# Latent attention's scores in a two-layer backbone: from 96-row products, head after head, to 64-row products of two heads side by side

## The chip, the cores and the metric

The kernel runs on one core of one Trainium2 chip. The metric is device time in microseconds for one execution; the time before is 1802.9 us, the median of three runs (1801.73 to 1808.01). Besides its five engines (PE multiplies matrices, DVE and ACT work on vectors, POOL is a slower vector engine, SP issues transfers) the text speaks of the tile shape of a matmul, as the trace writes it: `128*128` uses all 128 rows of the array for the contraction, `64*128` only one half of them, so that two such products can stand in it together.

## What is computed

A backbone of two layers over 512 latent tokens and 256 context tokens, width 1024. Each layer: a modulated norm, one input projection whose columns go to four groups (neighbourhood attention, sliding window attention, latent attention, state space), an output projection, then a modulated norm and an MLP of 4096 with squared ReLU. In the second layer the context stream is not carried on. Latent attention, cut to what matters (4 heads; 64 features without position, 32 rotary ones that all heads share on the key's side):

```python
cq, ckv, kr = split(p, [256, 384])
q  = rmsnorm(cq, g_q) @ w_uq            # per head: qn (64), qr (32)
kv = rmsnorm(ckv, g_kv) @ w_ukv         # per head: kn (64), v (64)
qr, kr = axial_rope(qr, ang), axial_rope(kr, ang)   # latent tokens only
s = (einsum('bqhd,bkhd->bhqk', qn, kn) + einsum('bqhd,bkd->bhqk', qr, kr)) * 96 ** -0.5
o = softmax(s) @ v                      # 128 queries at a time
```

## The kernel before

**Products in two parts.** To keep the accuracy of float32 with the faster number format, nearly every operand is split in a high and a low part (in the code `h` and `l`: `wh`, `wl`, `ah`, `al`), and a product is three matmuls: high by high, low by high, high by low. `dense()` does so for all projections and the MLP. It takes the weights of 128 output columns, splits them (high part on ACT, low part on DVE), and runs 8 matmuls for each of the three passes and each segment: segment 0 are the 512 latent tokens, segment 1 the 256 context tokens.

**Order.** The kernel is written in Python generators, one for each group, that are merged; a scheduler of the toolchain then orders each engine's instructions by its own estimates, except where `tc.issue_after` chains two. So the text of the program does not fix the place of an instruction. Banks for scores come from a pool (`pss`), those for transposes and dense products from another (`pst`).

**Latent attention** is `mla()`. It loads its weights by POOL's queue, norms `ckv` and `cq`, turns the rotary key (`krr`, all 32 features of a token beside each other), and then makes the queries in three blocks of 128 columns: two blocks hold two heads' position-free parts each, the third the rotary parts of all four heads (rows 32 by 32). Scaled copies on ACT and, for the rotary part, four 32-row additions on DVE put them in `qh[hd]`, one tile of 96 rows a head: 64 position-free, 32 rotary. The keys go the same way into `kh[hd]` and `kl[hd]`: the rotary key is transposed and written to rows 64 to 96 of all four heads, the position-free part to rows 0 to 64, each time by `put_k`, with a copy on ACT (high) and a subtraction on DVE (low). There are 16 of each in a layer. `split_q` makes high and low of the query block (ACT, POOL).

**A score block** is 128 queries of one head against the 512 latent and the 256 context keys (context queries, in the first layer only: 256 context keys). `attend()` takes the two heads of a pair together. For latent attention it runs all scores of the first head, then all of the second: three matmuls of 96 rows each for 512 and for 256 columns. For the other two attentions (`paired=True`) the heads' 64-row products alternate, chained with `issue_after`. Then, head by head: minimum over the scores on DVE, exponential on ACT, reciprocal and scaling; the probabilities are transposed by PE, 128 columns at a time (L473), copied, and multiplied with the values in a 128x64 shape (L479). A layer has two pairs of heads and 4 or (first layer) 6 blocks.

**The MLP's start.** The MLP begins for the latent half before the context half of the norm is through (in the second layer: for the first 256 tokens before the second 256). `rest` is the generator with what is left of output projection and norm; `NAHEAD` up blocks (3 and 5) are computed for the first half alone; in the middle of the first one, and a few times after each (`PACE`, 6), one step of `rest` is placed. Its last steps are the norm's: sums of squares (L296), the reciprocal root on DVE, the broadcast of it over the partitions (L308), and the modulation: `xn`, high part `ah`, low part `al` for each of the 8 tiles of 128 features.

Of the kernel before, what the change touches and what calls it, by code (L numbers as in the profile page):

```python
# [72 lines left out]
QORD = (0, 1, 2)  # L73
# [18 lines left out]
def kernel(ctx: ExitStack, tc: tile.TileContext, D: dict, out: bass.AP, dbg=None):  # L92
# [157 lines left out]
    def dense(src, acts, segs, evac, ks=range(KD), w=None, low=V, midway=None):  # L250
# [139 lines left out]
    def attend(q, k, parts, sinks, vt, put, sgn=-1.0, paired=False):  # L390
# [14 lines left out]
        if paired:  # L405


            off, prev = 0, None
            for k0, n, tab in parts:
                if off == 0 or off + n - b0 > 512:  # L410
                    banks, b0 = (pss(), pss()), off
                dst = [banks[a][:, off - b0:off - b0 + n] for a in range(2)]
                nmm = len(terms(0))
                for i in range(nmm):
                    for a in range(2):
                        x, y = terms(a)[i]
                        with (tc.issue_after(prev.ins) if prev else nullcontext()):
                            prev = PE.matmul(dst[a], x, y[:, k0:k0 + n], start=i == 0, stop=i == nmm - 1)  # L418
                for a in range(2):
                    ats[a].append((dst[a], off, n, tab))  # L420
                off += n
        else:
            for a in range(2):
                off = 0
                for k0, n, tab in parts:
                    if off == 0 or off + n - b0 > 512:
                        bank, b0 = pss(), off
                    dst = bank[:, off - b0:off - b0 + n]
                    mm = terms(a)
                    for i, (x, y) in enumerate(mm):  # L430
                        PE.matmul(dst, x, y[:, k0:k0 + n], start=i == 0, stop=i == len(mm) - 1)  # L431
                    ats[a].append((dst, off, n, tab))
                    off += n
# [205 lines left out]
    for l in range(DEPTH):  # L639
# [329 lines left out]
        def mla():  # L969
# [36 lines left out]
            for b in range(4):  # L1006
# [4 lines left out]
            qh = [unit("u", nm("qh")) for _ in range(4)]  # L1011
            kh = [(unit("u", nm("kh"), F32R), unit("u", nm("kl"), F32R)) if SR[2] else unit("u", nm("kh"))
                  for _ in range(4)]

            def put_k(hd, r0, r1, c0, n, ps):
                if not SR[2]:
                    evac(kh[hd][r0:r1, c0:c0 + n], ps)
                    return
                hi, lo = (x[r0:r1, c0:c0 + n] for x in kh[hd])
                A.copy(hi, ps)  # L1020
                V.tensor_tensor(lo, ps, hi.bitcast(F32), ALU.subtract)

            vm = [unit("u", nm("vm")) for _ in range(2)]

            def queries():
                msc = -(96.0 ** -0.5)
                for b in QORD:
                    for s, c0, n in segs:
# [4 lines left out]
                        if b < 2:  # L1033
                            for e in range(2):
                                A.activation(qh[2 * b + e][0:64, c0:c0 + n], ps[64 * e:64 * e + 64, :n], AF.Copy, scale=msc)
                        elif s == 1:
                            for hd in range(4):
                                A.activation(qh[hd][64:96, c0:c0 + n], ps[32 * hd:32 * hd + 32, :n], AF.Copy, scale=msc)
                        else:
                            qr, qs = unit("q", nm("qr")), unit("q", nm("qs"))  # L1040
                            A.activation(qr[:, :SEQ], ps, AF.Copy, scale=msc)
# [4 lines left out]
                            for hd in range(4):  # L1046
                                rs_ = slice(32 * hd, 32 * hd + 32)
                                V.tensor_tensor(qh[hd][64:96, 0:SEQ], qr[rs_, :SEQ], qs[rs_, :SEQ], ALU.add)
# [4 lines left out]
            for s, c0, n in full:  # L1053
                pk = pss()
                for t in range(n // P):
                    PE.transpose(pk[0:32, t * P:(t + 1) * P], krr[:, c0 // P + t, :], ident)
                for hd in range(4):
                    put_k(hd, 64, 96, c0, n, pk[0:32, 0:n])
            yield
            for b in range(2):  # L1060
                for s, c0, n in full:
                    ps = pss()
                    PE.matmul(ps[:, :n], wkv[:, b * P:(b + 1) * P], ckv[:, c0:c0 + n], start=True, stop=True)
                    for e in range(2):
                        put_k(2 * b + e, 0, 64, c0, n, ps[64 * e:64 * e + 64, :n])
# [8 lines left out]
            for b in range(2):  # L1074
                om = unit("u", nm("om"))
                for j in range(WS // P):
# [7 lines left out]
                    qs = [qh[2 * b + a][0:96, cs] for a in range(2)]  # L1084
                    ks = [kh[2 * b + a] for a in range(2)]
                    if SR[2]:
                        qs = [tuple(x[0:96] for x in split_q(x, 96)) for x in qs]
# [381 lines left out]
```

## Time and profile before

| what | value |
|---|---|
| median of 3 runs | 1802.9 us (1801.73 to 1808.01) |
| the profiled execution | 1802.71 us, of which the span 1800.9 |
| PE busy | 1750.6 us, 97% of the span |
| DVE, ACT, POOL busy | 1109.4, 737.8, 240.3 us |
| latent scores (L431) | 216 matmuls: 96 of 512 columns, 120 of 256 |

How to read it: a line of the timeline gives an instruction's start and length in us, then the engine, the line of the code, the operation, what it writes and reads, its tile shape and sizes, how many alike follow, and, in brackets, how long the engine was idle before it and what ended that. Matmuls are pipelined: one's start lies ahead of the end of the one before, so the price of one is the distance between two ends (start plus length) or between two starts, not its length. In the windows the granted clock is 1.00 for 2.4 GHz and 0.50 for 1.2 GHz.

### The profile page before, as it was taken

How to read it: one execution, taken by the hardware profiler on the slowest of the kernel's cores; microseconds unless marked ns; L12 is line 12 of the kernel's file. 1: busy time of each engine (PE TensorE's matmuls, PEld its weight loads, DVE VectorE, ACT ScalarE, POOL GpSimd, SP SyncE). 2: the span in 40 equal slices, each digit the busy share in tenths (PEclk: the TensorE clock that was granted, in tenths of full speed). 3: DMA queues.
4: the chain of work that ended last, by engine and by line, in shares of the span. 5: the costliest groups of instructions: out<-in, count | busy, mean ns of one | idle time of the engine just before them, and what ended most of it. 6: DMA issues, size and time to landing. Idle time of an engine off the chain costs nothing.

```text
span 1800.9 us, 28892 instructions
## 1 busy us (share of the span) xinstructions
PE 1750.6 (97%) x11170; PEld 1493.3 (83%) x11170; DVE 1109.4 (62%) x2372; ACT 737.8 (41%) x1497; POOL 240.3 (13%) x367
## 2 busy tenths in 40 slices
PE   8999999999989999999999999999989999999998
PEld 7877877777878888888888998688878898888888
DVE  5548458688677566467555674757779563444355
ACT  4347546655353123123123443545544451323244
POOL 0102011234320000000000331101114310000002
PEclk8999999999999999999999999899999999999999
DMA  9440267632635445344444534111333543222333
GB/s 337 138 152 17 67 214 248 214 115 93 211 109 177 136 153 163 109 154 144 155 135 146 173 113 138 35 36 36 120 110 104 199 146 100 94 94 94 106 104 119
DMA packets 86249, 238.94 MB, mean 133 GB/s; under 512 B 9200, under 2 KB 17392, under 8 KB 86112
## 3 DMA queue, kind: packets, MB, share of 16 engines
q1 hardware_dynamic: 74976, 208.57, 35.8%
q0 software_dynamic: 7104, 24.33, 3.8%
q10 hardware_dynamic: 4032, 4.20, 0.7%
q8 instruction: 88, 1.44, 0.3%
q14 instruction: 49, 0.40, 0.1%
HBM read 214.52 MB, written 22.54 MB: 132 GB/s over the span
## 4 chain that ended last, share of the span: by engine, by line
PE 89%; DVE 6%; DMA 2%; ACT 1%; issue 1%; POOL 0%; DVEq 0%; ACTq 0%; POOLq 0%; SPq 0%
PE pt L261 68%; PE pt L479 3%; PE pt L473 3%; PE pS L666 2%; PE pS L431 2%; PE pS L418 2%; PE pt L172 1%; PE pt L666 1%; PE pt L296 1%; PE pt L933 1%; PE pS L1031 1%; DVE pr L441 1%; DVE wl L239 1%; PE pt L864 0%; DMA old<-in_hT_dram 0%
## 5 line engine op out<-in xcount | busy, mean ns | idle before, releaser
L238 ACT CAST wh<-wr 128x1024 fp32r<-128x1024 f32 x206 | 215.9, 1049 | 403.0 <-PE pt L261 291.2
L239 DVE TENSOR_TENSOR wl<-wr,wh 128x1024 fp32r<-128x1024 f32 x206 | 253.9, 1233 | 100.5 <-ACT wh L238 96.0
L261 PE MATMUL pt<-ah,wh 128*128 128x512 f32 (+1 forms) x1304 | 275.0, 352 | 7.1 <-ACT ah L346 3.1
L261 PE MATMUL pt<-al,wh 128*128 128x512 f32 (+1 forms) x1304 | 269.5, 347 | 0.0
L261 PE MATMUL pt<-ah,wl 128*128 128x512 f32 (+1 forms) x1304 | 268.7, 348 | 0.0
L261 PEld LDWEIGHTS pt<-ah,wh 128*128 128x128 f32 x1304 | 213.3, 190 | 48.0 <-ACT ah L346 4.3
L261 PEld LDWEIGHTS pt<-ah,wl 128*128 128x128 f32 x1304 | 215.2, 191 | 31.4 <-issue 0.8
L261 PEld LDWEIGHTS pt<-al,wh 128*128 128x128 f32 x1304 | 212.9, 190 | 31.1 <-issue 2.4
L261 PE MATMUL pt<-hh,wh 128*128 128x256 f32 (+1 forms) x896 | 168.2, 330 | 0.0
L261 PE MATMUL pt<-hl,wh 128*128 128x256 f32 (+1 forms) x896 | 167.0, 329 | 0.0
L261 PE MATMUL pt<-hh,wl 128*128 128x256 f32 (+1 forms) x896 | 166.9, 329 | 0.0
L1291 DVE SCALAR_TENSOR_TENSOR h<-pt,mod,h 128x512 f32<-128x512 f32 (+1 forms) x112 | 66.3, 595 | 153.8 <-PE pt L261 153.6
L261 PEld LDWEIGHTS pt<-hh,wh 128*128 128x128 f32 x896 | 137.6, 189 | 17.7 <-issue 0.6
L261 PEld LDWEIGHTS pt<-hh,wl 128*128 128x128 f32 x896 | 138.0, 190 | 15.4
L261 PEld LDWEIGHTS pt<-hl,wh 128*128 128x128 f32 x896 | 138.1, 190 | 15.0
L208 DVE SCALAR_TENSOR_TENSOR ma<-wm,cact,ma 128x768 f32<-128x768 f32 x112 | 109.9, 1013 | 65.3 <-DMA wm<-in_w_mod_dram 65.2
L1281 ACT ACTIVATE r<-pt 128x512 f32<-128x512 f32 (+1 forms) x101 | 51.4, 509 | 237.1 <-PE pt L261 237.1
L1283 DVE TENSOR_TENSOR r<-r 128x512 f32<-128x512 f32 (+1 forms) x101 | 58.2, 577 | 123.0 <-ACT r L1281 122.9
L322 POOL TENSOR_TENSOR sq<-sq,sq 128x256 f32<-128x256 f32 x66 | 64.7, 980 | 442.9 <-ACT sq L318 442.2
L455 ACT ACTIVATE pr<-pr,m 128x512 f32<-128x512 f32 (+2 forms) x96 | 77.8, 811 | 40.3 <-DVE m L441 38.4
L261 PE MATMUL pt<-oh,wo 128*128 128x256 f32 (+1 forms) x576 | 93.9, 306 | 0.0
L261 PEld LDWEIGHTS pt<-oh,wo 128*128 128x128 f32 x576 | 79.0, 194 | 5.5 <-issue 1.7
(295 smaller groups left out, 2473.5 us busy)
## 6 DMA issues: line engine op xcount, KB each, us to landing
wr<-in_w_mlp_dram SPq DMA_DIRECT2D x154, 512.0 KB, 3.5
wo<-oscr SPq DMA_DIRECT2D x66, 512.0 KB, 4.7
wm<-in_w_mod_dram SPq DMA_DIRECT2D x80, 384.0 KB, 3.6
wr<-in_w_a_dram SPq DMA_DIRECT2D x36, 512.0 KB, 4.1
wm<-in_w_mod_dram SPq DMA_DIRECT2D x32, 512.0 KB, 4.0
wr<-in_w_out_dram SPq DMA_DIRECT2D x16, 512.0 KB, 4.3
oscr<-wh POOLq DMA_DIRECT2D x16, 512.0 KB, 3.7
oscr<-wl POOLq DMA_DIRECT2D x16, 512.0 KB, 5.6
```

What stands on the lines that cost most here:

```text
L208: V.scalar_tensor_tensor(a[:, :T], w, cact[:, k, i:i + 1], a[:, :T], ALU.mult, ALU.add)
L238: A.copy(wh, raw)
L239: low.tensor_tensor(wl, raw, wh.bitcast(F32), ALU.subtract)
L261: PE.matmul(ps[:, :n], w[:, k - k0, :], acts[k][a][:, c0:c0 + n], start=i == 0, stop=i == len(mm) - 1)
L322: G.tensor_tensor(sq[0][:, :n], sq[0][:, :n], q[:, :n], ALU.add)
L455: A.activation(pr[:, :off], src, AF.Exp, scale=-1.0 if tabs else sgn, bias=mcol, accum_out=s2[:, a:a + 1])
L473: PE.transpose(pt[:, i * P:(i + 1) * P], probs[a][:, (g0 + i) * P:(g0 + i + 1) * P], ident)
L479: last_mm = PE.matmul(pv[64 * a:64 * a + 64, :P], vt(a, t), pts[a][:, t * P:(t + 1) * P], start=t == 0, stop=t == nkt - 1)
L666: PE.matmul(acc[t], acts[k][a][:, t * P:(t + 1) * P], slabs[pc][w][:, kk, :], start=k == 0 and x == 0, stop=k == KD - 1 and x == 2)
L1281: A.activation(r[:, :n], ps, AF.Relu)
L1283: V.tensor_tensor(r2[:, :n], r[:, :n], r[:, :n], ALU.mult)
L1291: V.scalar_tensor_tensor(h[d][:, c0:c0 + n], ps, mod[:, 40 + d, s:s + 1], h[d][:, c0:c0 + n], ALU.mult, ALU.add)
```

## The change

The position-free parts of two heads stay as the projection gives them, side by side in 128 rows (`qn`, `kn`), and the product of a head reads its 64 rows. The rotary parts get a product of their own: for each head 64 rows that hold 32 of the query's high part above 32 of its low part (`qst`), against the key's high part twice (`kst[0]`) and its low part twice (`kst[1]`). So a block has five 64-row terms a head instead of three 96-row ones, and all attentions now run the paired form, the two heads alternating. `kst` comes from four copies of the rotary key beside each other (`k4`), transposed as 128x128. `qst` is put together by 8 transfers a layer on POOL's queue (`RQ = 0`). The rotary query block is made first (`QORD`). A further part is in the MLP's start: `midway` now names the matmul ahead of which a step of `rest` is placed, the first up block has its step at matmul 12 of 24, the second one at 6 (first layer) or 18 (second), and the steps after the first up block are gone.

```diff
-QORD = (0, 1, 2)
+QORD = (2, 0, 1)
+RQ = 0
 ...
-                if midway and i == len(mm) // 2:
-                    midway()
+                if midway and i == midway[0]:
+                    midway[1]()
 ...
-            return [(q[a][0], k[a][0]), (q[a][1], k[a][0]), (q[a][0], k[a][1])]
+            return [(q[a][0], k[a][0]), (q[a][1], k[a][0]), (q[a][0], k[a][1]), *extra[a]]
 ...
+            k4 = unit("q", nm("k4"))
+            A.copy(k4[:, :T].rearrange("p (t r e) -> p t r e", r=4, e=32),
+                   krr[:, :, None, :].to_broadcast([P, 6, 4, 32]))
+            for s, c0, n in full:
+                pk = pss()
+                for t in range(n // P):
+                    PE.transpose(pk[:, t * P:(t + 1) * P], k4[:, c0 + t * P:c0 + (t + 1) * P], ident)
+                hi, lo = (x[:, c0:c0 + n] for x in kst)
+                A.copy(hi, pk[:, 0:n])
+                V.tensor_tensor(lo, pk[:, 0:n], hi.bitcast(F32), ALU.subtract)
 ...
-                            for hd in range(4):
-                                rs_ = slice(32 * hd, 32 * hd + 32)
-                                V.tensor_tensor(qh[hd][64:96, 0:SEQ], qr[rs_, :SEQ], qs[rs_, :SEQ], ALU.add)
+                            V.tensor_tensor(qr[:, :SEQ], qr[:, :SEQ], qs[:, :SEQ], ALU.add)
+                    if b == 2:
+                        hi, lo = unit("q", nm("qrh"), F32R), unit("q", nm("qrl"), F32R)
+                        A.copy(hi[:, :WS], qr[:, :WS])
+                        V.tensor_tensor(lo[:, :WS], qr[:, :WS], hi[:, :WS].bitcast(F32), ALU.subtract)
+                        for hd in range(4):
+                            for i, x in enumerate((hi, lo)):
+                                r0 = 64 * (hd % 2) + 32 * i
+                                (G, nc.scalar)[RQ].dma_start(qst[hd // 2][r0:r0 + 32, :WS].bitcast(F32),
+                                                             x[32 * hd:32 * hd + 32, :WS].bitcast(F32))
 ...
-                    for e in range(2):
-                        put_k(2 * b + e, 0, 64, c0, n, ps[64 * e:64 * e + 64, :n])
+                    hi, lo = (x[:, c0:c0 + n] for x in kn[b])
+                    A.copy(hi, ps[:, :n])
+                    V.tensor_tensor(lo, ps[:, :n], hi.bitcast(F32), ALU.subtract)
 ...
-                    attend(qs, ks,
-                           part, None, vt, lambda ps, om=om, cs=cs: evac(om[:, cs], ps))
+                    x = split_q(qn[b][:, cs], P)
+                    attend([rows(x, a, slice(0, P)) for a in range(2)], [rows(kn[b], a) for a in range(2)],
+                           part, None, vt, lambda ps, om=om, cs=cs: evac(om[:, cs], ps),
+                           extra=[[(rows(qst[b], a, cs), rows(y, a)) for y in kst] for a in range(2)])
 ...
-                    ahead.append(up_block(qd, f, parts[:1], midway=None if f else lambda: next(rest)))
-                    for _ in range(PACE[l] - (f == 0)):
+                    now = (12, (6, 18)[last], None)[min(f, 2)]
+                    ahead.append(up_block(qd, f, parts[:1], midway=now and (now, lambda: next(rest))))
+                    for _ in range(PACE[l] if f else 0):
                         next(rest, None)
```

The line numbers after the change are a little other than before: L431 becomes L418, L473 L461, L479 L467, L261 L262, L296 L297, L308 L309, L1021 L1052 and L1014.

**PE, latent attention of the first layer, before**: the scores of one head (`kh`, `kl` by `nqh`, `nql`), between transposes of probabilities (`con,pr`) and the product with the values (`vm`).

```order
L473 MATMUL pt_1413<-con,pr_1394 128x128 x4
L473 MATMUL pt_1419<-con,pr_1394 128x128 x2
L1105 MATMUL pt_1440<-sq_1017,con 128x512
L431 MATMUL pS_1612<-kh_1109,nqh_1602 128x512
L431 MATMUL pS_1612<-kh_1109,nql_1603 128x512
L431 MATMUL pS_1612<-kl_1110,nqh_1602 128x512
L473 MATMUL pt_1487<-con,pr_1472 128x128 x4
L479 MATMUL pt_1419<-pT_1401,vm_1117 64x128
```

The same place after: the two heads' banks alternate, `kst,qst` are the rotary terms, and four transposes stand inside the fourth pair of terms, two more behind the fifth.

```order
L418 MATMUL pS_1596<-kh_1107,nqh_1590 128x512
L418 MATMUL pS_1597<-kh_1107,nqh_1590 128x512
L418 MATMUL pS_1596<-kh_1107,nql_1591 128x512
L418 MATMUL pS_1597<-kh_1107,nql_1591 128x512
L418 MATMUL pS_1596<-kl_1108,nqh_1590 128x512
L418 MATMUL pS_1597<-kl_1108,nqh_1590 128x512
L418 MATMUL pS_1596<-kst_1113,qst_1111 128x512
L461 MATMUL pt_1478<-con,pr_1459 128x128 x4
L418 MATMUL pS_1597<-kst_1113,qst_1111 128x512
L418 MATMUL pS_1596<-kst_1114,qst_1111 128x512
L418 MATMUL pS_1597<-kst_1114,qst_1111 128x512
L461 MATMUL pt_1484<-con,pr_1459 128x128 x2
```

Before, transposes stand between whole heads; now a pair of heads is one chain of ten for 512 columns, cut once inside by transposes and once ahead of the 256 columns.

**DVE, latent attention of the second layer, before**: behind the rotation of the query (`qs`, `qr`) come the additions into `qh` and then the keys' low parts, of which the first five are shown.

```order
L1044 TENSOR_TENSOR qs_11680<-pt_11682,sin_11442 128x512
L1045 TENSOR_TENSOR qr_11679<-qr_11679,cos_11441 128x512
L1048 TENSOR_TENSOR qh_11652<-qr_11679,qs_11680 32x512
L1048 TENSOR_TENSOR qh_11653<-qr_11679,qs_11680 32x512
L1048 TENSOR_TENSOR qh_11654<-qr_11679,qs_11680 32x512
L1048 TENSOR_TENSOR qh_11655<-qr_11679,qs_11680 32x512
L1021 TENSOR_TENSOR kl_11657<-pS_11749,kh_11656 32x512
L1021 TENSOR_TENSOR kl_11657<-pS_11762,kh_11656 32x256
L1021 TENSOR_TENSOR kl_11657<-pS_11783,kh_11656 64x512
L1021 TENSOR_TENSOR kl_11659<-pS_11749,kh_11658 32x512
L376 COPY sk_11690<-pt_11723 128x256
L1021 TENSOR_TENSOR kl_11659<-pS_11762,kh_11658 32x256
```

After: the rotary key's low parts (`kst`) come first, then one addition, the rotary query's low part (`qrl`), and four low parts of the keys.

```order
L1014 TENSOR_TENSOR kst_11675<-pS_11680,kst_11674 128x512
L1014 TENSOR_TENSOR kst_11675<-pS_11687,kst_11674 128x256
L1030 TENSOR_TENSOR qs_11693<-pt_11698,sin_11456 128x512
L1031 TENSOR_TENSOR qr_11692<-qr_11692,cos_11455 128x512
L1032 TENSOR_TENSOR qr_11692<-qr_11692,qs_11693 128x512
L1036 TENSOR_TENSOR qrl_11704<-qr_11692,qrh_11703 128x512
L377 COPY sk_11723<-pt_11756 128x256
L240 TENSOR_TENSOR wl_12260<-wr_12257,wh_12259 128x1024
L1052 TENSOR_TENSOR kl_11669<-pS_11782,kh_11668 128x512
L1052 TENSOR_TENSOR kl_11669<-pS_11786,kh_11668 128x256
L1052 TENSOR_TENSOR kl_11671<-pS_11790,kh_11670 128x512
L1052 TENSOR_TENSOR kl_11671<-pS_11794,kh_11670 128x256
```

Four additions became one, and of the 16 subtractions into `kl` four are left, with two into `kst` ahead of the rotation.

**PE, start of the MLP in the first layer, before**: sums of squares (L296) and broadcast (L308) of the norm's second half, between the dense matmuls of the first and second up block.

```order
L261 MATMUL pt_5991<-al_5662,wh_5987 128x512
L296 MATMUL pt_6004<-ones,sq_5825 128x1 x2
L261 MATMUL pt_5991<-al_5664,wh_5987 128x512
L308 MATMUL pt_6037<-con,rs_6009 128x128 x2
L261 MATMUL pt_6066<-ah_5649,wh_6062 128x512
L261 MATMUL pt_6066<-ah_5651,wh_6062 128x512
```

After: the second up block's matmuls stand between the two.

```order
L297 MATMUL pt_6018<-ones,sq_5839 128x1 x2
L262 MATMUL pt_6059<-ah_5663,wh_6055 128x512
...
L262 MATMUL pt_6059<-ah_5669,wh_6055 128x512
L262 MATMUL pt_6005<-al_5678,wh_6001 128x512
L262 MATMUL pt_6059<-ah_5671,wh_6055 128x512
...
L262 MATMUL pt_6059<-al_5676,wh_6055 128x512
L262 MATMUL pt_6059<-al_5678,wh_6055 128x512
L309 MATMUL pt_6066<-con,rs_6023 128x128 x2
L262 MATMUL pt_6127<-ah_5663,wh_6123 128x512
L262 MATMUL pt_6127<-ah_5665,wh_6123 128x512
```

One dense matmul stood between sums and broadcast; now there are 25, the one left of the first up block among them.

## Rows read from the trace of the kernel before

**Rows 1.** the page: busy time by engine, and the chain that ended last

```profile
PE 1750.6 (97%) x11170; PEld 1493.3 (83%) x11170; DVE 1109.4 (62%) x2372; ACT 737.8 (41%) x1497; POOL 240.3 (13%) x367
...
PE 89%; DVE 6%; DMA 2%; ACT 1%; issue 1%; POOL 0%; DVEq 0%; ACTq 0%; POOLq 0%; SPq 0%
```

**Rows 2.** timeline of PE, latent scores of layer 0: start us, length us, instruction

```profile
145.92 0.39 PE L431 MATMUL pS<-kh,nqh 96*128 96x512 f32 x1
...
146.62 0.28 PE L431 MATMUL pS<-kh,nqh 96*128 96x256 f32 x1
...
146.97 0.40 PE L431 MATMUL pS<-kh,nqh 96*128 96x512 f32 x1
...
148.10 0.88 PE L473 MATMUL pt<-con,pr 128*128 128x128 f32 x6
148.73 0.48 PE L431 MATMUL pS<-kh,nqh 96*128 96x512 f32 x1
```

**Rows 3.** timeline of PE, entry and exit of the 64-row tiles in layer 0

```profile
210.45 0.38 PE L418 MATMUL pS<-oh,nqh 64*128 64x256 f32 x1
210.76 0.44 PE L473 MATMUL pt<-con,pr 128*128 128x128 f32 x2
211.13 0.38 PE L418 MATMUL pS<-oh,nqh 64*128 64x256 f32 x1
...
211.71 0.39 PE L418 MATMUL pS<-ol,nqh 64*128 64x256 f32 x2
212.03 1.31 PE L473 MATMUL pt<-con,pr 128*128 128x128 f32 x10
...
227.63 0.27 PE L418 MATMUL pS<-oh,nqh 64*128 64x256 f32 x1
227.83 2.12 PE L261 MATMUL pt<-ah,wh 128*128 128x512 f32 x8
```

**Rows 4.** windows: us, busy us of each engine (instructions), granted clock, DMA share, GB/s

```profile
142.00:200.00 58.00, 57.76 (x450) 46.26 (x449) 46.36 (x141) 41.37 (x107) 13.37 (x28) 1.00 0.15 47
...
1126.00:1153.00 27.00, 24.98 (x92) 15.52 (x92) 17.73 (x28) 13.70 (x29) 2.51 (x7) 0.94 0.19 59
1153.00:1168.00 15.00, 13.31 (x56) 10.40 (x55) 14.88 (x42) 8.05 (x20) 2.85 (x5) 0.77 0.00 1
1425.00:1440.00 15.00, 11.20 (x64) 10.40 (x64) 10.53 (x28) 8.27 (x19) 6.57 (x7) 0.77 0.44 154
```

**Rows 5.** timeline of DVE, layer 1: the low parts of the keys

```profile
1140.87 2.44 DVE L1021 TENSOR_TENSOR kl<-pS,kh 32x512 fp32r<-32x512 f32 x4 [2.21 <-ACT kh L1020]
...
1145.51 5.69 DVE L1021 TENSOR_TENSOR kl<-pS,kh 64x512 fp32r<-64x512 f32 x10
```

**Rows 6.** timeline of PE, layer 1, between the keys and the first latent scores

```profile
1146.35 1.10 PE L1063 MATMUL pS<-ckv,wkv 128*128 128x512 f32 x2 [0.85 <-DVE kl L1021]
1148.46 0.71 PE L1063 MATMUL pS<-ckv,wkv 128*128 128x256 f32 x2 [1.02 <-DVE kl L1021]
```

**Rows 7.** timeline of PE, start of the MLP in layer 0

```profile
516.68 0.43 PE L308 MATMUL pt<-con,rs 128*128 128x128 f32 x2 [3.01 <-DVE rs L288]
516.87 3.18 PE L261 MATMUL pt<-ah,wh 128*128 128x512 f32 x8
...
525.84 1.98 PE L261 MATMUL pt<-ah,wl 128*128 128x512 f32 x8
527.65 1.98 PE L261 MATMUL pt<-al,wh 128*128 128x512 f32 x8
529.47 3.01 PE L261 MATMUL pt<-ah,wh 128*128 128x256 f32 x22
```

**Rows 8.** timeline of DVE, the second half's modulation, MLP of layer 0

```profile
517.23 1.66 DVE L339 SCALAR_TENSOR_TENSOR xn<-h,gsc,pt 128x256 f32<-128x256 f32 x4
...
533.17 0.48 DVE L347 SCALAR_TENSOR_TENSOR al<-xn,mod,ah 128x256 fp32r<-128x256 f32 x1
```

**Rows 9.** DMA issues: KB each, us from issue to landing

```profile
vscr<-vna POOLq DMA_DIRECT2D x12, 128.0 KB, 2.3
```

More of the change, by code (lines that the diff above doesn't have):

```diff
@@ L387, in behind, with attend @@
             fn()
-    def attend(q, k, parts, sinks, vt, put, sgn=-1.0, paired=False):
+    def attend(q, k, parts, sinks, vt, put, sgn=-1.0, extra=((), ())):
         tabs = len(parts) > 1
@@ L401, in terms @@
                 return [(q[a], k[a])]
-            return [(q[a][0], k[a][0]), (q[a][1], k[a][0]), (q[a][0], k[a][1])]
+            return [(q[a][0], k[a][0]), (q[a][1], k[a][0]), (q[a][0], k[a][1]), *extra[a]]
         ats = ([], [])
[L405 to L418, printed above, removed]
+        off, prev = 0, None
+        for k0, n, tab in parts:
+            if off == 0 or off + n - b0 > 512:
+                banks, b0 = (pss(), pss()), off
+            dst = [banks[a][:, off - b0:off - b0 + n] for a in range(2)]
+            nmm = len(terms(0))
+            for i in range(nmm):
                 for a in range(2):
-                    ats[a].append((dst[a], off, n, tab))
-                off += n
-        else:
+                    x, y = terms(a)[i]
+                    with (tc.issue_after(prev.ins) if prev else nullcontext()):
+                        prev = PE.matmul(dst[a], x, y[:, k0:k0 + n], start=i == 0, stop=i == nmm - 1)
             for a in range(2):
[L424 to L433, printed above, removed]
+                ats[a].append((dst[a], off, n, tab))
+            off += n
         for a in range(2):
@@ L1010, in mla @@
             V.tensor_copy(krr[:, 4:6], kr[:, 4:6])
[L1011 to L1021, printed above, removed]
-            vm = [unit("u", nm("vm")) for _ in range(2)]
+            qn = [unit("u", nm("qn")) for _ in range(2)]
+            kn = [(unit("u", nm("kh"), F32R), unit("u", nm("kl"), F32R)) for _ in range(2)]
+            qst = [unit("u", nm("qst"), F32R) for _ in range(2)]
+            kst = [unit("u", nm("kst"), F32R) for _ in range(2)]
+            vm = [unit("u", nm("vm")) for _ in range(2)]
+            k4 = unit("q", nm("k4"))
[8 more added lines that the diff above has]
+                V.tensor_tensor(lo, pk[:, 0:n], hi.bitcast(F32), ALU.subtract)
             def queries():
                 msc = -(96.0 ** -0.5)
+                qr, qs = unit("q", nm("qr")), unit("q", nm("qs"))
                 for b in QORD:
@@ L1032, in queries @@
                                       start=k == 0, stop=k == 1)
-                        if b < 2:
-                            for e in range(2):
-                                A.activation(qh[2 * b + e][0:64, c0:c0 + n], ps[64 * e:64 * e + 64, :n], AF.Copy, scale=msc)
-                        elif s == 1:
-                            for hd in range(4):
[L1038 to L1041, printed above, removed]
+                        dst = qn[b] if b < 2 else qr
+                        A.activation(dst[:, c0:c0 + n], ps[:, :n], AF.Copy, scale=msc)
+                        if b == 2 and s == 0:
                             pp = pst()
@@ L1052, in mla @@
                 yield from queries()
[L1053 to L1059, printed above, removed]
             for b in range(2):
@@ L1063, in mla @@
                     PE.matmul(ps[:, :n], wkv[:, b * P:(b + 1) * P], ckv[:, c0:c0 + n], start=True, stop=True)
-                    for e in range(2):
-                        put_k(2 * b + e, 0, 64, c0, n, ps[64 * e:64 * e + 64, :n])
+                    hi, lo = (x[:, c0:c0 + n] for x in kn[b])
+                    A.copy(hi, ps[:, :n])
+                    V.tensor_tensor(lo, ps[:, :n], hi.bitcast(F32), ALU.subtract)
             yield
@@ L1198, in put @@
                             evac(on[:, cs], ps)
-                    attend([rows(x, a, slice(0, P)) for a in range(2)], [rows(blocks["nk", b], a) for a in range(2)], part, None, vt, put, sgn=1.0, paired=True)
+                    attend([rows(x, a, slice(0, P)) for a in range(2)], [rows(blocks["nk", b], a) for a in range(2)], part, None, vt, put, sgn=1.0)
                     if j == 3:
```

10 lines of the change are left out of this document (1 added, 9 removed).

## Prediction

> **What bounds the kernel now.** I read the page first, then the stretches that the change touches. The page shows PE busy for 1750.6 of the span's 1800.9 us, and the chain that ended last is PE for 89% of its length, DVE for 6% [rows 1]: time is won or lost where PE's own work changes, or where PE waits. The windows then tell which it is in each stretch. During layer 0's latent attention (142 to 200 us) PE is busy 57.76 of 58 us at full clock, while DVE has 46.36 and ACT 41.37: only PE's work counts there. In layer 1, from the latent queries to the early scores (1126 to 1168), PE is busy 24.98 of 27 and 13.31 of 15, and its granted clock averages 0.94 and 0.77; DVE has 14.88 of the last 15 us [rows 4]. There DVE sets the pace, and PE pays twice, by waiting and by running at 1.2 instead of 2.4 GHz afterwards. Two of these waits are named: 0.85 and 1.02 us before the key matmuls, both ended by a low part of the keys (kl) on DVE [rows 6].
>
> **The scores: fewer PE slots.** A latent score block costs, per head, three 512-column and three 256-column matmuls, one after the other. By consecutive starts, three of 512 take 146.62 - 145.92 = 0.70 us, 0.233 each, and three of 256 take 146.97 - 146.62 = 0.35, 0.117 each [rows 2]. The program holds 96 of the first and 120 of the second: 96 x 0.233 + 120 x 0.117 = 36.4 us. Afterwards a pair of heads needs five pairs of 64-row matmuls (three latent terms, two rotary) in place of six single ones: 80 pairs of 512 and 100 pairs of 256. The trace has 64-row pairs of 256 columns: from the end at 211.51 to the end at 212.10 five pairs finish (the rows between are of the same kind, twelve matmuls in all), 0.118 a pair [rows 3]. So the two halves do run side by side, a pair costs what one 96-row matmul costs, and for 512 columns, which no row shows, I take 2 x 0.118 = 0.236 by the nearest row. The bounds are 0.233 (full overlap) and 0.467 (none). Sum: 80 x 0.236 + 100 x 0.118 = 30.7 us, that is -5.7. No overlap for 512 alone would turn this into +12.8; the 256 rows speak against it.
>
> **The scores: more changes of tile shape.** A 64-row tile differs from the 128-row one around it, and the trace prices that. Going in: transposes end at 211.20, the next 64-row matmul of 256 columns ends at 211.51, 0.31 against 0.118, so +0.19. Coming out: from 210.83 to 211.20 two transposes take 0.37, and from 212.10 to 213.34 ten take 1.24; eight more cost 0.87, so 0.109 each, and the exit is 0.37 - 0.22 = +0.15 [rows 3]. Into the dense product, eight matmuls after a 64-row one take 2.05 (227.90 to 229.95), against 1.81 (527.82 to 529.63) among themselves, +0.24 [rows 3, 7]. The 96-row scores of before don't pay it: transposes end at 148.98, the next score of 512 columns at 149.21, 0.23 later, its usual price [rows 2]. The TensorEngine Tiling (Array Packing) page of the Trainium skill, section Key Properties, says that changing the tiling mode drains the engine while changing the tile does not; the exits above agree.
>
> How many more there are the order tells, not the diff: entries from 128x128 into 64x128 go from 55 to 87, exits from 51 to 82, because the scheduler puts two or four transposes between score matmuls, even inside a term. 32 x 0.19 + 31 x 0.15 = +10.7 (with all exits at 0.24 it is +13.5). The rotary key's six transposes now run in the dense shape, 6 x 0.109 = 0.65 instead of 0.82 by before's row of the same stretch, which is 0.3 for both layers. PE's own work: -5.7 + 10.7 - 0.3 = +4.7. Layer 0's half of it is on the path in full, since PE is all that is busy there. With the pairs uncut (20 entries fewer) it would be about -2, with all exits dear about +7.5.
>
> **Layer 1's stretch: less on DVE.** Before, 16 subtractions make the keys' low parts in this layer: the four and ten in the rows, 2.44 + 5.69 us, and two of 256 columns, about 0.42 each by the shorter ones: 9.0 us [rows 5]. Four 32-row additions build the queries. After, four subtractions of 128 rows, two for the rotary key, one addition and one subtraction for the rotary query remain. DVE's price goes by columns: ten of mixed width averaged 0.57, so eight cost about 4.6 us. With the additions DVE loses roughly 7 us of work ahead of the first latent score. What PE can get back is bounded: idle 27 - 24.98 + 15 - 13.31 = 3.7 us, and the slow clock, (1 - 0.94) x 27 + (1 - 0.77) x 15 = 5.1 us, which is what running at half speed lost [rows 4]. So 0 to -8.8. I take the two waits named for kl, 1.9, the first drop of the clock that follows them, 1.6, and a quarter of the remaining 5.3: -5 in round numbers. The other waits are behind softmax, which stays.
>
> **The rotary query's copies.** Eight transfers on POOL's queue stack the query's high and low parts per layer; before has none. The nearest row, a write by the same queue, lands in 2.3 us [rows 9]. Queued behind them are the low parts of the latent queries on POOL. In layer 1's order there are 48 dense matmuls (24 x 0.227 + 24 x 0.12 = 8.3 us), the keys and the values between the rotary product and the first score that reads the stack, so I expect no wait: 0, at worst +3 in layer 1, nothing in layer 0, where sixty more matmuls stand between.
>
> **The MLP's start.** In layer 0 PE now waits 3.01 us for the reciprocal root before its broadcast (L308), then runs slow: the first eight matmuls take 3.18 us where eight later take 1.98, and the 48 from 516.87 to 529.47 need 12.6 us where 48 x 0.227 is 10.9, 1.7 lost [rows 7]. After, 25 dense matmuls stand ahead of the broadcast, so these 4.7 us go. But the second half's modulation, which starts with xn at 517.23, right after the broadcast, and ends with al at 533.65 [rows 8], comes later relative to PE: before, 48 matmuls of 512 columns run between broadcast and the first 256-column one at 529.47, after only 24 (24 x 0.227 = 5.45), plus 2.6 for the 22 that follow. PE reaches the last high part about 8.1 us after the broadcast; it came some 15 us after it, some 14 when one up block less is interleaved on DVE. New wait 5.8: net +1.1, between -4.7 (hidden after all) and +3 (and a new drop of the clock). Layer 1's start already idles, 3.8 of 15 us [rows 4], ahead of its broadcast; 77 matmuls then cover the second half: +0.5, 0 to 1.5.
>
> **Sum.** +4.7 - 5.0 + 0 + 1.1 + 0.5 = +1.3 against the profiled 1802.71 us (span 1800.9 and 1.8 around it), which stands 0.2 under the median of 1802.9: 1804.
>
> **Rivals.** First, clearly faster: layer 1's stretch gives back all 8.8, and the modulation's wait stays hidden (-4.7), with the shape changes partly falling into waits in layer 1 (+3 instead of +4.7): 1802.7 - 10.5 = 1792. For it: both waits are tied to DVE, which loses 7 us. Against it: layer 0 has nothing to hide the changes. The same page's Overview gives up to twice the speed for contraction sizes of 64 or less; five slots for six is all that this trace allows of it.
>
> Second, slower: the pairs delay softmax in layer 1. Before, the first head's scores are complete after 1.05 us (0.70 + 0.35) and its softmax begins while PE makes the second head's; after, both are complete only at 5 x 0.354 = 1.77. Where DVE is saturated (14.88 of 15) and PE has no dense work ready, the chain of each block starts 0.7 later, 8 blocks in layer 1: +5.8, and the -5 doesn't come. 4.7 + 5.8 + 1.1 + 0.5 = +12: 1815. It decides where PE waits after scores for transposes; for it, the stretch is already softmax-bound at its end; against it, the second head is ready 0.3 sooner. The tiling page's section PSUM Bottleneck says that tiling speeds the engine but not the emptying of its banks, by which this rival would be right in layer 1; layer 0's free DVE speaks against it there.
>
> Third, the modulation's wait is worse than costed and drops the clock again, with PE's work at +7.5: 1811, inside the range.
>
> **How the numbers follow.** A measurement of this kernel can tell about 0.5%, 9 us, from no change (1793.9 to 1811.9). My forecast with its own range, 1796 to 1811, gets 0.52; the faster rival 0.25; the slower one 0.16, the third 0.07. Faster by over 0.5%: 0.25; slower by more: 0.16 and a share of the third's, 0.22; within: 0.53. The range from 1791 to 1815 holds all but the far ends.
>
> **What would show it.** Right: latent pairs of 512 columns about 0.236 apart; the first matmul after each change 0.15 to 0.24 longer; the stretch in layer 0 from first to last latent score longer by 2 to 5 us; the waits behind kl gone and the first latent score of layer 1 about 5 us sooner after its queries; at the MLP's start of layer 0 no wait before the broadcast, and new ones for ah or al in the 256-column products. Wrong: a wait of the first rotary score for a transfer, 512-column matmuls that run one after the other, or a clock that drops at new places.

## The result: slower by 0.9%

The changed kernel takes 1819.87 us (median of four, 1817.88 to 1824.49) against 1803.65 for the kernel before in the same series: ratio 1.009, 95% interval 1.0062 to 1.0118. I had forecast 1804 with a range from 1791 to 1815. The profiled execution took 1817.88, its span is 1816.1, 15.2 longer than before.

The page of the changed kernel, busy times and chain (answers to [rows 1]): PE is busy only 8 us longer (more work, or work at the low clock), DVE 12 us less. The other 7 of the 15 us must be waiting.

```profile
PE 1758.8 (97%) x11314; PEld 1492.3 (82%) x11314; DVE 1097.5 (60%) x2348; ACT 720.5 (40%) x1452; POOL 233.9 (13%) x363
...
PE 88%; DVE 7%; DMA 3%; issue 1%; ACT 1%; POOL 0%; DVEq 0%; ACTq 0%; POOLq 0%; SPq 0%
```

Cut at the first and last matmul of a kind, the two traces differ in few places (us; a stretch that starts with the queries and ends with the first latent score is called the way to the first score below):

| stretch | before | after | change | forecast |
|---|---|---|---|---|
| layer 0, first to last latent score | 57.0 | 72.1 | +15.1 | +2 to +5 |
| layer 0, first output product to first down product (MLP's start within) | 225.1 | 229.4 | +4.3 | +1.1 |
| layer 1, first query matmul to first latent score | 27.6 | 21.4 | -6.2 | -5 |
| layer 1, first to last latent score | 67.3 | 71.1 | +3.8 | half of +4.7 |
| all the rest | | | -1.8 | +0.5 |

The windows over these stretches, before and then after (us, then busy us of PE, PEld, DVE, ACT, POOL with instructions, granted clock, DMA share, GB/s):

```profile
142.60:199.50 56.90, 56.66 (x445) 45.32 (x444) 45.69 (x139) 40.47 (x105) 13.12 (x27) 1.00 0.14 46
1126.00:1153.60 27.60, 25.59 (x95) 15.85 (x95) 18.27 (x30) 14.19 (x30) 2.51 (x7) 0.94 0.19 57
1153.60:1220.90 67.30, 65.61 (x435) 55.20 (x433) 45.83 (x119) 35.44 (x74) 8.50 (x15) 0.95 0.11 32
```

```profile
141.70:213.80 72.10, 65.42 (x549) 46.98 (x547) 47.02 (x139) 38.44 (x93) 7.43 (x16) 0.95 0.14 45
1145.60:1167.00 21.40, 21.40 (x86) 14.47 (x86) 10.16 (x17) 7.97 (x18) 5.88 (x12) 1.00 0.33 99
1167.00:1238.10 71.10, 69.15 (x524) 54.35 (x523) 44.96 (x114) 32.71 (x68) 4.14 (x10) 0.98 0.10 31
```

In layer 0's stretch PE was busy for 56.66 of 56.9 us before; now it is busy 65.42 of 72.1, at a mean clock of 0.95. So waits appeared where PE had been all that counted. In layer 1 the way to the first score is now all PE, at full clock, with DVE at 10.16 instead of 18.27.

**The wait in layer 0.** PE's timeline there (start us, length us, instruction, in brackets the idle time ahead and what ended it):

```profile
141.72 0.50 PE L418 MATMUL pS<-kh,nqh 64*128 64x512 f32 x2
142.06 0.40 PE L418 MATMUL pS<-kh,nql 64*128 64x512 f32 x2
142.29 0.39 PE L418 MATMUL pS<-kl,nqh 64*128 64x512 f32 x2
142.52 0.62 PE L418 MATMUL pS<-kst,qst 64*128 64x512 f32 x4
...
144.26 0.84 PE L418 MATMUL pS<-kh,nqh 64*128 64x512 f32 x2 [0.53 <-DVE mx L429]
...
145.17 0.85 PE L418 MATMUL pS<-kst,qst 64*128 64x512 f32 x4
149.43 1.25 PE L418 MATMUL pS<-kh,nqh 64*128 64x256 f32 x2 [3.40 <-DVE m L429]
```

The first block runs as forecast. The second one waits 0.53 us for DVE's minimum over the first block's context scores (`mx`), and then 3.40 us for the one over the latent scores (`m`, L429). Matmuls after that are long: the clock is at 1.2 GHz from 147.9 to 154.8. What DVE and ACT did meanwhile:

```profile
147.48 1.23 DVE L240 TENSOR_TENSOR wl<-wr,wh 128x1024 fp32r<-128x1024 f32 x1 [2.93 <-ACT wh L239]
148.62 0.74 DVE L429 CUSTOM_DVE_ANT_0 pr<-pS,zero,mx 128x512 f32<-128x512 f32 x1
```

```profile
146.40 1.04 ACT L239 CAST wh<-wr 128x1024 fp32r<-128x1024 f32 x1 [6.97 <-DMA wr<-in_w_a_dram]
147.35 0.29 ACT L952 CAST nqh<-qn 128x128 fp32r<-128x128 f32 x1
149.41 0.93 ACT L443 ACTIVATE pr<-pr,m 128x768 f32<-128x768 f32 x1 [1.76 <-DVE m L429]
```

DVE was not busy, it waited 2.93 us in front of a weight's low part (wl), and with it everything behind, the softmax of the first block included: its last latent score ended at 143.14, and the minimum over these scores began only at 148.62, right behind wl. The low part waited for the high part (wh) on ACT, and ACT for the weight's transfer, 6.97 us. The block's exponential and the next query's split stood behind that cast. The weight itself is for a product 50 us later (197.51). SP's queue shows why it came late, after and then before:

```profile
115.30 4.24 SPq L170 DMA_DIRECT2D wm<-in_w_mod_dram  x2
141.83 0.33 SPq L245 DMA_DIRECT2D wr<-in_w_a_dram  x1
```

```profile
116.88 3.02 SPq L169 DMA_DIRECT2D wm<-in_w_mod_dram  x2
120.23 0.69 SPq L244 DMA_DIRECT2D wr<-in_w_a_dram  x1
```

The load was issued at 141.83 instead of 120.23, right after the end (141.79) of this group on PE:

```profile
140.74 1.05 PE L173 MATMUL pt<-wm,cact 128*32 128x512 f32 x4
```

These matmuls read the modulation's weights, which lie in the same pool of three buffers as the projections' weights (`wr`). The scheduler has put this group of four behind two dense products and all keys and values, immediately ahead of the first score; before, the last such group in front of the scores ended at 119.53. That the group held the buffer is read from the code and from these two times; no run moved the group by itself.

**The MLP's start in layer 0.** Answers to [rows 7]:

```profile
534.73 0.38 PE L309 MATMUL pt<-con,rs 128*128 128x128 f32 x2
...
538.59 1.98 PE L262 MATMUL pt<-al,wh 128*128 128x512 f32 x8
540.40 0.87 PE L262 MATMUL pt<-ah,wh 128*128 128x256 f32 x6
542.25 0.62 PE L262 MATMUL pt<-ah,wh 128*128 128x256 f32 x3 [0.97 <-ACT wh L239]
544.27 2.29 PE L262 MATMUL pt<-ah,wh 128*128 128x256 f32 x9 [1.40 <-ACT ah L344]
548.01 1.01 PE L262 MATMUL pt<-ah,wh 128*128 128x256 f32 x3 [1.46 <-ACT ah L344]
549.77 0.58 PE L262 MATMUL pt<-ah,wh 128*128 128x256 f32 x1 [0.74 <-ACT ah L347]
550.15 1.91 PE L262 MATMUL pt<-ah,wl 128*128 128x256 f32 x8
```

The wait for the root is gone, as forecast, and the new waits stand where they were forecast, in the 256-column products, for wh and ah: 0.97 + 1.40 + 1.46 + 0.74 = 4.6 us. What the sum had left out is the clock: 1.2 GHz from 543.9 to 554.1, so eight matmuls of 256 columns need 1.91 us.

### The profile page after: what moved, and what is told of

It is laid out like the page before. It is cut to its first block, busy times and chain, and to the rows that moved or that the text cites. A ratio compares the mean times of both kernels' runs of the same rounds, so it can differ in the third digit from the quotient of the medians.

```text
span 1816.1 us, 29107 instructions
## 1 busy us (share of the span) xinstructions
PE 1758.8 (97%) x11314; PEld 1492.3 (82%) x11314; DVE 1097.5 (60%) x2348; ACT 720.5 (40%) x1452; POOL 233.9 (13%) x363
## 3 DMA queue, kind: packets, MB, share of 16 engines
q8 instruction: 89, 1.46, 0.3%
## 4 chain that ended last, share of the span: by engine, by line
PE 88%; DVE 7%; DMA 3%; issue 1%; ACT 1%; POOL 0%; DVEq 0%; ACTq 0%; POOLq 0%; SPq 0%
PE pt L262 67%; PE pS L418 3%; PE pt L467 3%; PE pt L461 3%; PE pS L654 2%; PE pt L173 1%; PE pt L654 1%; PE pt L297 1%; DVE pr L429 1%; PE pS L1023 1%; PE pt L921 1%; PE pt L852 1%; DVE wl L240 1%; DVE xn L340 1%; DMA wr<-in_w_a_dram 0%
## 5 line engine op out<-in xcount | busy, mean ns | idle before, releaser
L262 PE MATMUL pt<-ah,wh 128*128 128x512 f32 (+1 forms) x1304 | 279.4, 355 | 12.0 <-ACT ah L344 5.3
L262 PE MATMUL pt<-al,wh 128*128 128x512 f32 (+1 forms) x1304 | 269.7, 347 | 0.0
L262 PE MATMUL pt<-ah,wl 128*128 128x512 f32 (+1 forms) x1304 | 269.3, 349 | 0.0
L262 PEld LDWEIGHTS pt<-ah,wh 128*128 128x128 f32 x1304 | 215.4, 192 | 56.0 <-ACT ah L344 6.6
L262 PEld LDWEIGHTS pt<-ah,wl 128*128 128x128 f32 x1304 | 216.2, 193 | 31.0 <-issue 0.5
L262 PEld LDWEIGHTS pt<-al,wh 128*128 128x128 f32 x1304 | 213.2, 190 | 30.8 <-issue 1.9
L262 PE MATMUL pt<-hh,wh 128*128 128x256 f32 (+1 forms) x896 | 168.2, 330 | 0.0
L262 PE MATMUL pt<-hl,wh 128*128 128x256 f32 (+1 forms) x896 | 167.0, 329 | 0.0
L262 PE MATMUL pt<-hh,wl 128*128 128x256 f32 (+1 forms) x896 | 166.9, 329 | 0.0
L262 PEld LDWEIGHTS pt<-hh,wh 128*128 128x128 f32 x896 | 137.6, 189 | 17.7 <-issue 0.6
L262 PEld LDWEIGHTS pt<-hh,wl 128*128 128x128 f32 x896 | 138.0, 190 | 15.4
L262 PEld LDWEIGHTS pt<-hl,wh 128*128 128x128 f32 x896 | 138.1, 190 | 15.0
L262 PE MATMUL pt<-oh,wo 128*128 128x256 f32 (+1 forms) x576 | 92.9, 304 | 0.0
L461 PE MATMUL pt<-con,pr 128*128 128x128 f32 x512 | 79.8, 284 | 3.6 <-DVE pr L450 1.3
```

The lines of the kernel that those rows point to most:

```text
L461: PE.transpose(pt[:, i * P:(i + 1) * P], probs[a][:, (g0 + i) * P:(g0 + i + 1) * P], ident)
```

## The experiments

Ratios are against the kernel before on the same chip, which had medians of 1804.4 to 1805.2 there. Where the intervals of two ratios overlap, the whole times don't tell the two kernels apart, and the reading rests on the stretches, each from one trace.

**split_late: the late split behind the first softmax.** In layer 0, splits of weights traced late in latent attention are chained behind the second block's softmax; one weight is moved by it.

```diff
-        A.copy(wh, raw)
-        low.tensor_tensor(wl, raw, wh.bitcast(F32), ALU.subtract)
+        with (tc.issue_after(gate[0]) if gate else nullcontext()):
+            A.copy(wh, raw)
+        with (tc.issue_after(gate[1]) if gate else nullcontext()):
+            low.tensor_tensor(wl, raw, wh.bitcast(F32), ALU.subtract)
...
+                    if l == 0 and (b, j) == (0, 1):
+                        first2 = [x.ins for x in soft]
+                    if l == 0 and (b, j) == (1, 2):
+                        gate[:] = first2
```

> The changed kernel, with one weight's split (wh on ACT, wl on DVE) in layer 0 put behind the softmax of the first two latent blocks. Theory (the split waits for a late transfer, and softmax is queued behind it): the waits of 0.53 and 3.40 us at the second block and the slow clock at 148 to 155 us go, the latent stretch of layer 0 shrinks from 72.1 to 63-66 us, the whole to 1810-1814 us. Rival (the pairs themselves delay softmax, since both heads need all four banks): the stretch stays at 70-73 us, the whole at 1818-1821.

Measured: 1814.88, ratio 1.0055 (1.0036 to 1.0074); the stretch falls to 64.6 us, at full clock:

```profile
143.90:208.50 64.60, 61.70 (x521) 44.25 (x520) 46.06 (x136) 36.65 (x87) 7.16 (x13) 1.00 0.16 50
```

The theory holds for the wait of 3.40 us and the slow clock, which are gone; the wait of 0.53 us stayed, so it is not the split's, and the whole came out just above the 1810 to 1814 expected. The stretch is 7.5 of the 15.1 us shorter. PE is now busy 61.70 us, 5.0 more than before; 2.9 are waits of 0.3 to 0.5 us for softmax. So what is left of the loss, 64.6 - 57.0 = 7.6, is 5.0 of work and 2.7 of waits that before did not have (it had 0.2).

These stretches don't hold quite the same work: in the changed kernel a block's 24 value products and 8 modulation matmuls more fall into it than in split_late. From the first latent query product to the first output product the two do the same work. The windows over that longer stretch of layer 0, before, changed and split_late:

```profile
107.50:356.20 248.70, 243.97 (x1689) 189.15 (x1687) 162.75 (x413) 147.53 (x350) 39.91 (x84) 1.00 0.45 151
107.70:371.50 263.80, 253.55 (x1763) 191.03 (x1761) 155.98 (x400) 136.77 (x320) 34.93 (x80) 0.98 0.43 144
109.90:367.10 257.20, 251.65 (x1761) 188.97 (x1760) 155.15 (x399) 136.38 (x320) 35.64 (x80) 0.99 0.45 148
```

By them the change costs 15.1 us here too, and the one split was 6.6 of these.

**pair96: pairing without 64-row tiles.**

```diff
-                           part, None, vt, lambda ps, om=om, cs=cs: evac(om[:, cs], ps))
+                           part, None, vt, lambda ps, om=om, cs=cs: evac(om[:, cs], ps), paired=True)
```

> The kernel before, with the latent scores of the two heads alternating as one chain, still 96 rows each and three terms, so with the pairing but without 64-row tiles: six slots a block, no changes of tile shape for them. Theory (the tile shapes cost, the pairing does not): the latent stretch of layer 0 stays at 56-58 us and that of layer 1 at 66-69, the whole within 3 us of before. Rival (both heads' scores ready together delay softmax): layer 0's stretch 60 us or more, layer 1's 70 or more, the whole 5 to 10 us above before.

Measured: 1806.26, ratio 1.0016 (1.0003 to 1.0028); the windows over the two latent stretches:

```profile
143.50:201.30 57.80, 56.51 (x444) 45.15 (x443) 45.10 (x138) 39.29 (x102) 11.46 (x27) 1.00 0.12 39
1157.20:1224.20 67.00, 64.85 (x432) 55.04 (x432) 43.75 (x113) 32.98 (x71) 6.76 (x14) 0.95 0.11 33
```

57.8 and 67.0 us against 57.0 and 67.3, PE busy 56.51 and 64.85. So that both heads' scores come together costs little: 1.1 us more of waits in layer 0 (57.8 - 56.51 = 1.3 against 0.2), none in layer 1, and 0.16% of the whole. My second rival falls. PE's work does not grow; what it has more in the changed kernel goes with the 64-row terms and their changes of shape, not with the pairing.

**uncut_late: fewer changes of shape by force.**

```diff
+        lead = tc.issue_after(anchors[-2]) if extra[0] and len(anchors) >= 2 else nullcontext()
...
-                        with (tc.issue_after(prev.ins) if prev else nullcontext()):
+                        with (tc.issue_after(prev.ins) if prev else lead):
```

> As split_late, and each latent score block waits on PE for the value product of the block two before, so that fewer transposes stand inside a block's chain: 397 changes of tile shape instead of 418. Theory (each entry and exit costs what the trace of before showed): PE's own work falls by 5 to 6 us against split_late, 1804-1809. Rival (the order costs as much in waits for softmax as it saves in changes): 1810-1816.

Measured: 1824.83, ratio 1.0108 (1.0091 to 1.0125), 10 us slower than split_late. The window over layer 0's stretch, which now holds more dense work (645 matmuls against 521):

```profile
143.30:227.30 84.00, 75.26 (x645) 57.44 (x645) 52.12 (x148) 44.07 (x103) 7.16 (x16) 0.96 0.18 57
```

8.7 us without work on PE against 2.9, and the clock drops. Over the longer stretch, where the work is that of split_late:

```profile
109.20:370.20 261.00, 248.55 (x1763) 189.37 (x1761) 156.70 (x400) 137.10 (x320) 34.47 (x80) 0.99 0.44 146
```

PE's work did fall, by 3.1 us, with 40 entries into 64 rows there against 47 (7 entries and exits at 0.19 + 0.15 would be 2.4), so the price of the changes is borne out. But PE's idle time rose from 5.6 to 12.5 us, so layer 0 lost 3.8 us. Most of the loss lies in layer 1, which from its first latent query product to its first output product takes 200.3 us against 193.1. The rival holds, and more strongly than it said: the transposes that cut the chains are what PE does while it waits for softmax.

**old_mid and mid_alone: the MLP's start.** The first is the changed kernel with the old placing, the second the kernel before with the new one.

```diff
-                    now = (12, (6, 18)[last], None)[min(f, 2)]
+                    now = None if f else 12
...
-                    for _ in range(PACE[l] if f else 0):
+                    for _ in range(PACE[l] - (f == 0)):
```

> The changed kernel with the MLP's start as before (one step of the rest in the middle of the first up block, five steps behind it). Theory (the later broadcast makes the second half's modulation late, waits of 4.6 us and 10 us at the low clock): 4 us of the stretch from the last output product to the first down product come back, 1815-1817 us. Rival (the second layer loses what the first one gains, or the old wait for the root of 3 us comes back in full): 1818-1821.

> The kernel before with the new start of the MLP alone. Theory: +4 us against before, 1806-1809, with waits for ah in the 256-column products of layer 0's MLP start and a slow clock behind them. Rival (the lateness came from the shifted stage ahead): 1802-1805.

Measured: old_mid 1817.45, ratio 1.0065 (1.0045 to 1.0084); from the last output product to the first down product of layer 0 78.4 us instead of 82.1, with the wait of 3.01 for the root back. Of the 3.7 us layer 1 loses 1.8 (from its first latent query product to the end 672.3 us against 670.5), and the whole lies between the two that were expected. mid_alone 1806.86, ratio 1.0007 (0.9993 to 1.002), no difference that this can tell; the stretch is 80.7 against 78.1, and its trace has the waits of 0.97, 1.40, 1.46 and 0.75 us and the low clock (525.9 to 536.1), but the two drops at 507 and 517 us of before are missing. So the placing does cause the new waits, and is dearer in the changed kernel (3.7) than alone (2.6), less than the 4 I expected.

**late_old: both repairs.** The edits of split_late and old_mid together.

> The changed kernel with both repairs: the late split behind the first softmax in layer 0 and the old start of the MLP. Theory (the two add up): 1809-1812 us, still 4 to 8 above before, since the changes of tile shape stay. Rival (they don't add up, because what one frees the other loses): 1813-1816.

Measured: 1811.75, ratio 1.004 (1.0027 to 1.0053). They add up, at the upper end of what was expected; the stretches are 64.6 and 78.3 us, and the interval lies clear below that of the changed kernel. This trace also prices what is left in layer 0, since its clock stays full from the first latent query product to the first output product (110.7 to 366.7): 256.0 us, 7.3 more than before, of which PE is busy 250.16, 6.2 more. There are 27 more entries into 64 rows than before, and as many exits: 27 x (0.19 + 0.15) = 9.2, less 3.1 for layer 0's share of the slots saved and about 0.7 for the rotary key's six transposes, which are now made ahead of this stretch, is 5.4. So the prediction's prices account for most of the work.

**pieces and pieces_both: layer 1's load on DVE, and on ACT.** PE's work as in the changed kernel, with DVE's (then ACT's too) work in layer 1 in the old 64- and 32-row pieces.

```diff
-                V.tensor_tensor(lo, pk[:, 0:n], hi.bitcast(F32), ALU.subtract)
+                for r in ([slice(32 * i, 32 * i + 32) for i in range(4)] if last else [slice(0, P)]):
+                    V.tensor_tensor(lo[r], pk[r, 0:n], hi[r].bitcast(F32), ALU.subtract)
```

> The changed kernel with layer 1's low parts of the keys and the rotation's addition on DVE in the old pieces (64 and 32 rows): 16 subtractions and four additions as before, in place of six and one; PE's work as in the changed kernel. Theory (layer 1's 6.2 us from the queries to the first latent score came from DVE's lighter load): 21.4 us become 25-28, the whole 3 to 6 us above the changed kernel. Rival (they came from the order, the keys' transposes ahead of the queries): 21-22.5 us, the whole unchanged.

> The changed kernel with layer 1's copies on ACT in the old pieces too (high parts of keys and rotary key, scaled queries), beside the pieces on DVE. The pieces on DVE alone lengthened the way from the queries to the first latent score by 1.4 of the 6.2 us in question. Theory (banks come free only after ACT and then DVE are through their pieces, so both loads together make the wait): 24.5-28 us, and the whole 3 to 6 us above the kernel with pieces on DVE alone. Rival (the order did the rest: the rotary keys' transposes and their splitting ahead of the queries, out of the stretch where DVE is full): 22-24 us, the whole within 2 us of it.

Measured: 1823.05, ratio 1.0106 (1.0084 to 1.0128), and 1826.89, ratio 1.0132 (1.0111 to 1.0153). The windows of pieces, the way to the first score and the stretch of latent scores; then those of pieces_both:

```profile
1148.20:1171.10 22.90, 22.24 (x88) 14.21 (x88) 17.86 (x29) 7.94 (x18) 5.84 (x12) 1.00 0.32 93
1171.10:1245.00 73.90, 68.84 (x524) 54.13 (x523) 45.98 (x116) 32.84 (x68) 3.29 (x10) 0.98 0.09 29
```

```profile
1144.60:1168.50 23.90, 22.61 (x86) 14.10 (x86) 17.62 (x29) 14.26 (x30) 5.85 (x12) 1.00 0.30 89
1168.50:1241.80 73.30, 69.05 (x524) 54.60 (x524) 46.09 (x116) 32.78 (x68) 3.72 (x10) 0.98 0.09 30
```

DVE gets back 17.86 - 10.16 = 7.7 us of work, so the 7 us that I had worked out were there. But the way grows by only 1.5 us, with ACT's pieces by 2.5, of the 6.2; the scores' stretch by 2.8 and 2.2. My theory falls for the larger part of the way: DVE's load was behind 1.5 us of it (22.9 and 23.9 us lie in or near what the rivals expected). The order has a part in the rest: a rotation product of the next attention, 0.85 us, no longer stands ahead of the scores, and the rotary key's six transposes, about 0.7 us, are now made ahead of the queries. No run separates what is left. Over the whole of layer 1's latent attention, from the first query product to the first output product, DVE's load does carry the gain: 196.7 us before, 192.8 in the changed kernel, and 197.0 and 198.3 with the pieces.

**relief: DVE relieved while the scores stay.** The kernel before; in layer 1 the rotary key's low part is made once and copied by POOL, which also makes the four additions.

```diff
+                    if last and hd:
+                        A.copy(kh[hd][0][64:96, c0:c0 + n], pk[0:32, 0:n])
+                        G.tensor_copy(kh[hd][1][64:96, c0:c0 + n], kh[0][1][64:96, c0:c0 + n])
+                        continue
...
-                                V.tensor_tensor(qh[hd][64:96, 0:SEQ], qr[rs_, :SEQ], qs[rs_, :SEQ], ALU.add)
+                                (G if last else V).tensor_tensor(qh[hd][64:96, 0:SEQ], qr[rs_, :SEQ], qs[rs_, :SEQ], ALU.add)
```

> The kernel before with DVE relieved in layer 1 in another way, scores as before: the rotary key's low part is made once and copied to the other three heads by POOL, and POOL makes the four additions into the queries. Theory (DVE sets the pace of that stretch): from the queries to the first latent score 21-25 us instead of 27.6, the whole 2 to 6 us below before. Rival (POOL's slower instructions take DVE's place): 27-30 us, the whole at or above before.

Measured: 1805.17, ratio 1.0007 (0.9994 to 1.0021): no difference. The way is 25.3 us, 2.3 shorter, just short of the 21 to 25 that the theory has, but the profiled execution loses 5 us in layer 1's neighbourhood attention, with a wait of 1.35 us for a transfer and an additional drop of the clock; whether that goes with the edit stays open.

**hybrid: the change in layer 1 alone.** `latent = (mla if last else mla_old)()`, with the unpaired branch kept for layer 0, and the old MLP's start.

> Layer 0's latent attention and the MLP's start as before, layer 1's latent attention as in the changed kernel. PE's order is that of before up to layer 1. Theory (the change loses in layer 0, where PE alone is busy, and gains in layer 1, where it takes work off DVE): from the queries to the first latent score 21-22 us, the latent stretch of layer 1 70-73, the whole 2 to 5 us below before, 1799-1803. Rival (layer 1's gain is eaten there by the changes of tile shape, as its own stretch is 4 us longer): 1803-1808.

Measured: 1800.3, ratio 0.9978 (0.9964 to 0.9991): faster than the kernel before, by 4 us, as expected. The windows: layer 0's stretch, layer 1's way and its scores:

```profile
143.40:200.40 57.00, 56.76 (x445) 45.39 (x444) 45.95 (x139) 40.55 (x105) 12.74 (x27) 1.00 0.15 46
1127.10:1148.50 21.40, 21.40 (x86) 14.49 (x86) 10.17 (x17) 7.97 (x18) 5.86 (x12) 1.00 0.34 98
1148.50:1219.70 71.20, 69.25 (x524) 54.46 (x524) 44.95 (x114) 32.76 (x68) 4.10 (x10) 0.98 0.10 31
```

Layer 0 is as before, layer 1 as after. With the runs of pieces: the change is worth its price only where it takes work off an engine that PE waits for.

## Why the prediction was wrong

- **The step that failed** is "Layer 0's half of it is on the path in full, since PE is all that is busy there", with "2 to 5 us" for the stretch. It took the stretch to stay free of waits because it was so before. But with the change a group of four modulation matmuls came to stand at the end of the queue ahead of the scores, by the two times above these held the buffer of the next weight, and that weight's split stood ahead of softmax on ACT and DVE. The split's place cost 6.6 to 7.5 us (split_late), the slow clock included. The sum had no term for a wait in layer 0. I had read PE's order and DVE's for layer 1, but not, for layer 0, what stands ahead of the first softmax on ACT and DVE, and by which transfer that is released.
- **The shapes' price was right, the number too small.** Pairs of 512 columns end at 142.22, 142.46, 142.68 and, two more, 143.14: 0.23 each, forecast 0.236. Into 64 rows: from 141.79 to 142.22 is 0.43, so +0.20. But I counted only changes between 128x128 and 64x128. With those from and to the value products and the modulation, entries rise from 70 to 108 in the order, by 38 instead of 32, and in the latent stretches alone by 22 and 17, while elsewhere some fall away. The sum of 4.7 for both layers, and so 2.4 for layer 0, was 6.2 in layer 0 by itself (late_old, at full clock), and about 3.5 in layer 1's stretch (69.15 against 65.61 busy, at different clocks and with a block's value products more in it).
- **The MLP's start** went by the mechanism, waits of 4.6 us against 5.8; mis-sized was the sum, since the low clock after the waits was kept for the range's end: +4.0 instead of +1.1.
- **Layer 1's way to the first score** came out (-6.2 against -5), and the relief of DVE was 7.7 against 7. But that the number came out is partly luck: the runs give DVE 1.5 of the 6.2, and 0.85 and 0.7 are work that only moved. Over layer 1's whole latent attention 3.9 us were gained, and DVE's pieces take all of it back.
- **Rivals.** The first, faster, had layer 1 give back 8.8 and the modulation's wait hidden; neither came. The second named slower, and the place was wrong: pairing costs nothing in layer 1 (pair96). The third had the MLP's mechanism and 1811; it took no wait in layer 0 either. No wait for the rotary query's copies showed in either layer, as forecast: they land in 2.2 us (median).

## What to carry over

Where one engine is full and nothing else waits, a change that moves instructions has to be read on the other queues too: look at what stands just ahead of the first dependent instruction in each engine's order, and at the transfer and the buffer that release it. Count every change of tile shape in the stretch itself, not in the program as a whole. And try a rewrite layer by layer: the same edit lost where PE was the limit and gained where PE waited for DVE.

## What was not expected of the hardware

During a wait of 3.4 us on PE the clock fell for 6.9 us to 1.2 GHz (147.9 to 154.8), and amid waits of 0.7 to 1.5 us in a row for 10.2 us (543.9 to 554.1), though none of these was longer than 1.5 us. PE was busy for 5.3 and 7.6 us of these, and at half speed half of that is lost: about 2.6 us on top of a wait of 3.4, and 3.8 on top of waits of 4.6.
